# First two units of three feed-forwards by eight plain products, and shorter pauses in the table work

## The chip, the cores and the metric

The kernel runs on one core of a Trainium2 chip. Its time is the device time of one execution in microseconds (us). TensorE does the matrix products, VectorE and ScalarE the elementwise work, GpSimd (POOL in the profile) elementwise work and the accumulating DMAs, SyncE (SP) issues the plain weight loads.

## The reference

The reference is one inference step of a backbone with two layers, on 512 latent and 128 context tokens of width 1024, in float32. Each layer is a gated feed-forward, a token mixing and a second gated feed-forward, each behind a norm that is scaled and shifted by a modulation:

```
h = modulate(rmsnorm(x, g1), sh1, sc1);  x = x + 0.5 * gate1 * ((silu(gate) * up) @ w_out),  gate, up = split(h @ w_in)
h = modulate(rmsnorm(x, gm), sh2, sc2);  x = x + gate2 * token_mixing(h)
h = modulate(rmsnorm(x, g3), sh3, sc3);  x = x + 0.5 * gate3 * ffn2(h)
```

The hidden width is 2816. The mixing holds attention, a spatial gate and a state space model whose tables (powers of a complex decay, products with B and C) depend on weights alone.

## The kernel before

**Products.** Tokens lie along the free axis in two tiles, A (320 to 639) and B (0 to 319); rows of 128 features lie on the partitions. Each float32 operand is split into a high part (ScalarE, line 199 for weights) and a low part (VectorE, line 207). `mm3` makes one product of a 128x128 weight tile and 320 tokens by three matmuls (lines 623 to 625) and advances a clock of its own, `T`, by 0.41. This clock is counted while the program is written out; it orders instructions and is no time of the chip. `K.run` goes through a list of tasks, loads weights ahead into 24 slots (line 174, SP's queue), adds two weight tiles where an operand is a sum (an accumulating load from GpSimd's queue, line 189) and splits them when they are due.

**A feed-forward.** It has 22 units (128 gate and 128 up columns each) in four or six blocks: BLOCKS gives blocks of 4, 4, 4, 3, 3, 4 units for the first feed-forward of a layer and of 6, 6, 6, 4 for the second. A unit needs a 2x2 block product: weights (gate, up) by input halves (features 0 to 3, 4 to 7), times inputs of tiles A and B. It is made by seven block products of four `mm3` each instead of eight. They need sums of the inputs of A and B: X["11"] and X["21"] are the two feature halves of A, "22" is the second half of B, and "t1" to "t4" are sums over both tiles. After a block's units come its output products (`out_task`), for all eight output tiles and both token tiles; in the last block tile A's are done before tile B's last six.

**The start of a feed-forward.** While A's operands are made by `norm`, B's (`later_operands`, `sums`) need A's. To cover that, the first four units (EARLY) begin with the two products that need A only (`early_task`): products with "11" into a bank, a copy of the bank (line 982), further products with "12" into the same bank. For these products the weights are loaded and split once more. The very first feed-forward, (0,0), is opened differently: its first two units go by eight plain products (`lead_task`, `lead_rest`), and the sums are made afterwards from the finished high and low parts of tile B (`all_x_sums`).

**Work beside the products.** Generators in `self.bg` emit instructions between products. Each yields a pause; `clock` advances a generator when `T` has passed its due time, ones that aren't `hot` only while no hot one (a norm, the sums) is alive. Two of them matter: `ada`, which makes the modulation on VectorE, and `ssm_build`, which makes the tables of the state space model during a layer's first feed-forward. `ssm_build` pauses at its start (line 1182), has a prelude, then works through four quarters of two directions each, on VectorE (CL, lines 1297 to 1304), GpSimd (EP and the angles T, lines 1123 to 1142 and 1335 to 1354), TensorE (lines 1315, 1328) and ScalarE (1330), stores to DRAM from GpSimd's queue, and copies a strip eight times at the end of each quarter (1362). When the last output product of tile A is written out, `done()` advances `ssm_build` to its end at once; then the next stage's norm for A is started, then tile B's last 24 products follow.

Of the kernel before, what the change touches and what calls it, by code (L numbers as in the profile page):

```python
# [20 lines left out]
KD = 8  # L21
# [5 lines left out]
HT = 320  # L27
# [31 lines left out]
class Kernel:  # L59
    def __init__(self, ctx, tc, a, o, depth=NL, stop=None, dbg=None):  # L60
# [11 lines left out]
        self.uid = 0  # L72
        self.stage = "in"
# [354 lines left out]
    def norm(self, l, i, X):  # L428
# [19 lines left out]
        if plain and X == "B":  # L448
            yield from self.later_operands(l, i, pb, pbs)
            return  # L450
# [15 lines left out]
        for n in range(KD + 1):  # L466
            yield 1.3
            jobs = []
            if n < KD:
                k = ks[n]  # L470
                t = xn.pop(n) if n in xn else dest(k)
                if plain:
                    name = PLAIN[X][k // 4]
                    hi, lo = self.xop(name) if name else (None, None)
                    hi, lo = (hi[:, k % 4], lo[:, k % 4]) if name else (None, None)
                else:
                    hi, lo = self.h(0, k, slice(s, e)), self.h(1, k, slice(s, e))
                for (r0, r1, c) in RANGES[X]:
# [5 lines left out]
                    else:  # L484
                        v.scalar_tensor_tensor(t[:, r], self.x[:, k, r0:r1], sc, pb[:, r], op0=ALU.mult, op1=ALU.mult)
                        if plain:
                            nc.scalar.activation(t[:, r], t[:, r], AF.Identity, bias=sh)
                        else:
                            nc.scalar.activation(hi[:, r], t[:, r], AF.Identity, bias=sh)
                            jobs.append((lo[:, r], t[:, r], sh, hi[:, r].bitcast(F32)))  # L490
                if n in VIA_POOL or plain and name:
                    if hi is not None:
                        nc.scalar.activation(hi, t, AF.Copy)
                        jobs.append((lo, t, 0.0, hi.bitcast(F32)))
# [4 lines left out]
            if not plain:  # L499
                self.ready[X] = n  # L500
            elif n:
                k = ks[n - 1]
                name = PLAIN[X][k // 4]
                if name:
                    self.xr[name] = k % 4 + 1
# [10 lines left out]
    def later_operands(self, l, i, pb, pbs):  # L516

        nc, v, g = self.nc, self.nc.vector, self.nc.gpsimd
        s, e = HALF["B"]
        m = self.mod[l]  # L520
        raw = {}
        (r0, r1, c), = RANGES["B"]

        def mod(k):
            return (m[:, c, (3 * i + j) * KD + k:(3 * i + j) * KD + k + 1] for j in (1, 0))

        def ahead(k):
            if k < 4:
                raw[k + 4], raw[k] = (self.spare("xn")[:, :HT] for _ in range(2))
                g.tensor_tensor(raw[k + 4], self.x[:, k + 4, s:e], pbs, op=ALU.mult)  # L530

        def first(k):
            t = raw[k]
            sc, sh = mod(k)
            v.scalar_tensor_tensor(t, self.x[:, k, s:e], sc, pb[:, :HT], op0=ALU.mult, op1=ALU.mult)
            nc.scalar.activation(t, t, AF.Identity, bias=sh)
            sc, sh = mod(k + 4)
            nc.scalar.activation(raw[k + 4], raw[k + 4], AF.Identity, bias=sh, scale=sc)
            nc.scalar.activation(self.xop("22")[0][:, k], raw[k + 4], AF.Copy)

        def low(k):
            hi, lo = (z[:, k] for z in self.xop("22"))
            v.tensor_tensor(lo, raw[k + 4], hi.bitcast(F32), op=ALU.subtract)
            self.xr["22"] = k + 1

        while self.norms["A"] in self.bg:
            self.advance(self.norms["A"])
        ahead(0)
        ahead(1)
        yield from self.sums(raw, first, low, ahead)  # L550

    def sums(self, raw, first, low, ahead):
# [14 lines left out]
        for k in range(4):  # L567
# [11 lines left out]
            low(k)  # L579
# [253 lines left out]
    def ffn_items(self, l, f, nxt, bg, lead=False):  # L833
# [19 lines left out]
        def start_bg():  # L853
# [3 lines left out]
            for mk in bg:  # L857
                work.append(self.spawn(mk(stack)))
# [320 lines left out]
    def ssm_build(self, l, p):  # L1179
# [85 lines left out]
        for qq in range(4):  # L1265
# [93 lines left out]
            for jj in range(8):  # L1359
                if jj % 2 == 0:  # L1360
                    yield 2.0
# [661 lines left out]
```

## Time and profile before

| | us |
|---|---|
| median of 3 runs | 2691.12 (2679.48 to 2693.58) |
| profiled execution | 2688.18 |
| its span | 2686.4 |
| TensorE busy | 2403.6 (89%) |
| VectorE busy | 1946.8 (72%) |
| ScalarE busy | 1121.4 (42%) |
| GpSimd busy | 1031.9 (38%) |

The span runs from the first to the last instruction of one profiled execution. Busy shares are means over all stages. The stages are seen by the tiles and lines: the feed-forward (0,0) lasts from about 70 to 611 us, the mixing of layer 0 to 929, (0,1) to 1392, (1,0) to 1925, the second mixing to 2229, and (1,1) to the end.

### The profile page before, as it was taken

The numbers are of one execution on the slowest core, as the hardware profiler recorded it, in microseconds if no ns is written. First come the engines' busy times: TensorE is split into PE (matmuls) and PEld (weight loads), VectorE is DVE, ScalarE is ACT, GpSimd is POOL, SyncE is SP. The second block draws the span as 40 slices with busy tenths as digits, with TensorE's granted clock in tenths as the row PEclk, the third lists the DMA queues.
The fourth block names the chain that finished last, engine by engine and source line by source line (L and its number), as shares of the span: only waits on it lengthen the run. The fifth ranks groups of instructions, "written<-read, shape, count | busy, mean of one in ns | idle before, by whom it ended". The sixth has DMA issues, their size and how long they took to land. (4 is left out here: it accounts for less than half of the span.)

```text
span 2686.4 us, 46513 instructions
## 1 busy us (share of the span) xinstructions
PE 2403.6 (89%) x16420; PEld 2315.5 (86%) x16420; DVE 1946.8 (72%) x4341; ACT 1121.4 (42%) x2567; POOL 1031.9 (38%) x1915
## 2 busy tenths in 40 slices
PE   6789999937999879999997999999498997999999
PEld 5689998837887779999996898899498886999999
DVE  7899788845857787777778987796466578655555
ACT  5433433414444553535354333335244446443533
POOL 5313665573533341211133365665633335121210
PEclk8899999968999989999998999999699998999999
DMA  6576777724453256866745676776153324664753
GB/s 217 135 190 175 183 189 193 188 64 131 147 159 100 75 127 184 192 188 164 193 135 140 163 191 174 183 197 155 52 167 118 111 66 95 143 144 121 157 124 98
DMA packets 197613, 398.19 MB, mean 148 GB/s; under 512 B 32274, under 2 KB 51826, under 8 KB 197380
## 3 DMA queue, kind: packets, MB, share of 16 engines
q1 hardware_dynamic: 132484, 255.46, 29.3%
q0 software_dynamic: 64896, 139.76, 26.8%
q8 instruction: 130, 2.13, 0.3%
q14 instruction: 103, 0.84, 0.1%
HBM read 372.48 MB, written 23.17 MB: 147 GB/s over the span
## 5 line engine op out<-in xcount | busy, mean ns | idle before, releaser
L623 PE MATMUL mm<-hx,w 128*128 128x320 f32 x2904 | 932.0, 321 | 110.3 <-ACT hid L982 27.8
L624 PE MATMUL mm<-hx,w 128*128 128x320 f32 x2904 | 920.9, 317 | 24.2 <-DVE hx L797 11.9
L625 PE MATMUL mm<-hx,w 128*128 128x320 f32 x2904 | 919.8, 317 | 6.3 <-DVE w L207 6.1
L207 DVE TENSOR_TENSOR w<-w 128x512 fp32r<-128x512 f32 (+1 forms) x922 | 628.6, 692 | 212.7 <-ACT w L199 209.0
L199 ACT ACTIVATE w<-w 128x512 fp32r<-128x512 f32 (+1 forms) x922 | 534.4, 608 | 489.5 <-DVE w L207 209.4
L623 PEld LDWEIGHTS mm<-hx,w 128*128 128x128 f32 x2904 | 562.8, 194 | 131.0 <-ACT hid L982 29.7
L624 PEld LDWEIGHTS mm<-hx,w 128*128 128x128 f32 x2904 | 563.7, 194 | 30.0 <-DVE hx L797 13.1
L625 PEld LDWEIGHTS mm<-hx,w 128*128 128x128 f32 x2904 | 563.2, 194 | 11.0 <-DVE w L207 10.5
L623 PE MATMUL mm<-hid,w 128*128 128x320 f32 x1408 | 442.0, 314 | 23.9 <-DVE x L661 20.2
L624 PE MATMUL mm<-hid,w 128*128 128x320 f32 x1408 | 438.6, 312 | 2.3 <-DVE hid L890 2.1
L625 PE MATMUL mm<-hid,w 128*128 128x320 f32 x1408 | 437.6, 311 | 0.0
L189 POOL DMA_DIRECT2D w<-f1i x176 | 152.7, 990 | 605.9 <-DVE w L207 377.9
L371 DVE SCALAR_TENSOR_TENSOR aj<-ar,sbc 128x1024 bf16<-128x1024 f32 x256 | 314.1, 1227 | 19.0 <-DMA ar<-w_ada 18.3
L661 DVE SCALAR_TENSOR_TENSOR x<-mm,mod,x 128x192 f32<-128x192 f32 (+1 forms) x576 | 232.3, 433 | 116.8 <-PE mm L625 115.9
L623 PEld LDWEIGHTS mm<-hid,w 128*128 128x128 f32 x1408 | 267.3, 190 | 31.2 <-DVE x L661 19.5
L189 POOL DMA_DIRECT2D w<-f0i x168 | 156.6, 1030 | 318.3 <-DVE w L207 260.8
L624 PEld LDWEIGHTS mm<-hid,w 128*128 128x128 f32 x1408 | 267.3, 190 | 4.3 <-DVE hid L890 4.2
L625 PEld LDWEIGHTS mm<-hid,w 128*128 128x128 f32 x1408 | 267.1, 190 | 0.0
L912 ACT ACTIVATE hid<-hid 128x320 f32<-128x320 f32 x158 | 74.6, 472 | 202.9 <-DVE hid L938 148.7
L886 ACT ACTIVATE hid<-hid 128x320 fp32r<-128x320 f32 x176 | 82.7, 471 | 153.3 <-DVE hid L954 76.1
L1803 PE MATMUL mm<-w,hx 128*128 128x256 f32 x480 | 144.2, 301 | 0.0
L1804 PE MATMUL mm<-w,hx 128*128 128x256 f32 x480 | 137.7, 287 | 0.9 <-DVE w L207 0.9
(347 smaller groups left out, 3213.1 us busy)
## 6 DMA issues: line engine op xcount, KB each, us to landing
ar<-w_ada SPq DMA_DIRECT2D x128, 512.0 KB, 4.9
w<-f1i SPq DMA_DIRECT2D x184, 256.0 KB, 4.4
w<-f0i SPq DMA_DIRECT2D x182, 256.0 KB, 4.1
w<-f1i POOLq DMA_DIRECT2D x176, 256.0 KB, 5.2
w<-f0i POOLq DMA_DIRECT2D x168, 256.0 KB, 5.6
w<-f1o SPq DMA_DIRECT2D x96, 192.0 KB, 2.5
w<-f0o SPq DMA_DIRECT2D x64, 256.0 KB, 4.3
w<-wqkv SPq DMA_DIRECT2D x48, 256.0 KB, 4.3
```

Of the source, the lines that this page charges most:

```text
L189: nc.gpsimd.dma_start(raw[r][:, :n], src, accum_op=ALU.add)
L199: nc.scalar.activation(pair[c][0][:, :n], raw[r][:, :n], AF.Copy)
L207: nc.vector.tensor_tensor(lo[:, :n], raw[r][:, :n], hi[:, :n].bitcast(F32), op=ALU.subtract)
L371: nc.vector.scalar_tensor_tensor(jk, r, 1.0, self.sbc[:, c, :], op0=ALU.mult, op1=ALU.mult, accum_out=m[:, c, j * KD + k:j * KD + k + 1])
L623: nc.tensor.matmul(out, hi, rhs_hi, start=start, stop=False, skip_group_check=parts)
L624: nc.tensor.matmul(out, hi, rhs_lo, start=False, stop=False, skip_group_check=parts)
L625: nc.tensor.matmul(out, lo, rhs_hi, start=False, stop=stop, skip_group_check=parts)
L661: nc.vector.scalar_tensor_tensor(self.x[:, m, r0:r1], p[:, r0 - s:r1 - s], self.mod[l][:, c, g * KD + m:g * KD + m + 1], self.x[:, m, r0:r ...
L886: nc.scalar.activation(hid[u, X][0], tmp[src], AF.Copy, scale=sign)
L912: return lambda: nc.scalar.activation(t, t, AF.Silu)
L1803: nc.tensor.matmul(p[:, :256], hh, wh, start=k == 0, stop=False)
L1804: nc.tensor.matmul(p[:, :256], hh, wl, start=False, stop=False)
```

## The change

Three parts, which come together:

1. In the feed-forwards other than (0,0), the first two units of the first block are made by eight block products each, as four tasks: tile A with the first half of the features, A with the second, B with the first, B with the second. In each task the order is feature tile by feature tile, two units by two columns into four banks. EARLY stays at four, counted from the third unit (two in blocks of four). 
2. `norm` makes all eight tiles of B as it makes A's (the first four in the place that later holds "t3"). The sums are made by `all_x_sums` from the finished parts, once the last plain task is begun (`self.whole`); `later_operands` is gone.
3. The pauses of `ssm_build` are multiplied by 0.77, and some are shortened besides: the first of layer 0 from 50 to 40, one from 1.5 to 0.5 in each direction, and at the end of a quarter 4.0 and four times 2.0 become 2.5 and once 1.5.

```
         if plain and X == "B":
-            yield from self.later_operands(l, i, pb, pbs)
-            return
...
+        if plain and X == "B":
+            while not self.whole:
+                yield 0.4
+            yield from self.all_x_sums()
...
             for mk in bg:
-                work.append(self.spawn(mk(stack)))
+                work.append(self.spawn(0.77 * (STEP if w is None else w) for w in mk(stack)))
...
+        def plain_items(us):
+            ps = {}
+            def part(X, h):
+                def fn(w):
+                    done = unit_done(us, X)
+                    self.whole = (X, h) == ("B", 1)
+                    if h == 0:
+                        ps[X] = [self.ps()[:, :HT] for _ in w]
+                    def mm(n, k):
+                        hi, lo = self.lead_x(X, k)
+                        self.mm3(ps[X][n], w[n], slice(k % 4 * 128, k % 4 * 128 + 128), hi, lo, k == 0, k == KD - 1)
+                    for k in range(4 * h, 4 * h + (4 if h == 0 else 2)):
+                        while self.ready[X] < min(KD, k + 3):
+                            self.advance(self.norms[X])
+                        for n in range(len(w)):
+                            mm(n, k)
+                    if h:
+                        while self.ready[X] < KD:
+                            self.advance(self.norms[X])
+                        for n in range(len(w)):
+                            for k in (KD - 2, KD - 1):
+                                mm(n, k)
+                            done(n, ps[X][n])
+                return fn
+            return [("task", [("fi", l, f, u, f"{r}{h + 1}") for u in us for r in "12"], part(X, h), 8 * len(us) * MM3[HT])
+                    for X in "AB" for h in range(2)]
...
                 items.append(("call", lambda: self.enter("in")))
-                units(us, us[:n_early] if b == 0 else [])
+                if b == 0:
+                    items += plain_items(us[:2])
+                    us = us[2:]
+                units(us, us[:EARLY] if b == 0 else [])
...
-        yield 50.0 if l == 0 else 12.0
+        yield 40.0 if l == 0 else 12.0
...
-                yield 1.5
+                yield 0.5
                 T = p.tile([128, 2, 2, 65], F32, tag="T", name="T")
...
-            yield 4.0
+            yield 2.5
             for jj in range(8):
-                if jj % 2 == 0:
-                    yield 2.0
+                if jj == 4:
+                    yield 1.5
```

## Rows read from the trace of the kernel before

**Rows 1.** The page: span, and busy us (share of the span) by engine.
```profile
span 2686.4 us, 46513 instructions
...
PE 2403.6 (89%) x16420; PEld 2315.5 (86%) x16420; DVE 1946.8 (72%) x4341; ACT 1121.4 (42%) x2567; POOL 1031.9 (38%) x1915
```

**Rows 2.** Windows, second matmul of each product alone (L624): stretch, length, PE busy (count).
```profile
552.00:635.00 83.00, 12.82 (x34) 8.38 (x35) 0.61 0.17 52
1883.60:1942.30 58.70, 10.19 (x29) 6.53 (x29) 0.65 0.20 59
929.90:985.20 55.30, 21.85 (x60) 14.11 (x61) 0.75 0.46 94
1392.40:1445.20 52.80, 19.71 (x52) 12.58 (x52) 0.74 0.40 81
2229.60:2285.10 55.50, 21.90 (x64) 13.83 (x64) 0.82 0.48 100
1390.00:1397.00 7.00, 2.99 (x9) 1.60 (x8) 0.95 0.44 97
2300.00:2660.00 360.00, 252.52 (x818) 153.41 (x817) 1.00 0.57 131
1530.00:1860.00 330.00, 211.42 (x676) 128.99 (x676) 0.98 0.72 184
210.00:552.00 342.00, 218.32 (x702) 133.05 (x701) 0.99 0.70 185
```

**Rows 3.** Timeline of TensorE around both ends: start, duration, instruction, [idle before, releaser].
```profile
551.65 0.31 PE L625 MATMUL mm<-hid,w 128*128 128x320 f32 x1
...
595.30 0.64 PE L1315 MATMUL sA<-CL,bbd 128*32 128x128 f32 x4 [20.36 <-DVE CL L1300]
...
623.16 0.64 PE L623 MATMUL mm<-hx,w 128*128 128x320 f32 x1 [11.68 <-ACT hx L489]
...
1908.23 0.64 PE L1315 MATMUL sA<-CL,bbd 128*32 128x128 f32 x4 [18.79 <-DVE CL L1300]
```

**Rows 4.** Timeline of GpSimd: the table work of layer 0.
```profile
345.97 1.30 POOL L1191 DMA_DIRECT2D BC<-sBC  x1
...
459.68 0.94 POOL L1191 DMA_DIRECT2D BC<-sBC  x1
...
554.39 1.79 POOL L1341 COPY T<-ang 128x2 f32<-128x2 f32 x12
...
613.52 4.09 POOL L1362 DMA_DIRECT2D dT<-dst  x8
```

**Rows 5.** Waits of TensorE, 929 to 980 us: total, times, longest.
```profile
PE mm L623 <- ACT hid L982: 9.6, 2, 6.6
PE mm L623 <- ACT hx L560: 5.4, 2, 3.5
...
PE sA L419 <- DVE acc L413: 1.1, 1, 1.1
```

**Rows 6.** Windows, all instructions: PE, PEld, DVE, ACT, POOL busy, PEclk, DMA share, GB/s.
```profile
1530.00:1860.00 330.00, 313.82 (x2100) 307.19 (x2099) 268.91 (x543) 131.42 (x272) 200.41 (x434) 0.98 0.72 184
```

**Rows 7.** Timelines of VectorE and TensorE: the sums of the opening.
```profile
97.90 2.36 DVE L607 TENSOR_TENSOR xn<-hx 128x320 f32<-128x320 f32 x4
...
119.40 0.63 PE L623 MATMUL mm<-hx,w 128*128 128x320 f32 x1 [3.21 <-ACT hx L560]
```

**Rows 8.** Groups by line on GpSimd, 1530 to 1860 us: busy, mean ns, idle before.
```profile
L189 POOL DMA_DIRECT2D w<-f0i x61 | 57.6, 1043 | 79.9 <-DVE w L207 62.7 <-DMA w<-f0i 6.4 <-DVE hid L933 5.9
L1341 POOL COPY T<-ang 128x2 f32<-128x2 f32 x72 | 19.7, 608 | 0.0
```

**Rows 9.** Waits of GpSimd, 1530 to 1860 us: total, times, longest.
```profile
POOL dT L1332 <- ACT ET L1330: 21.3, 5, 9.1
POOL dT L1308 <- DVE CL L1304: 15.3, 5, 6.3
```

More of the change, by code (lines that the diff above doesn't have):

```diff
@@ L72, in __init__ @@
         self.uid = 0
+        self.whole = False
         self.stage = "in"
@@ L447, in norm @@
         plain = i != 1
-        if plain and X == "B":
-            yield from self.later_operands(l, i, pb, pbs)
-            return
         ks = range(KD)
@@ L472, in norm @@
                 if plain:
-                    name = PLAIN[X][k // 4]
-                    hi, lo = self.xop(name) if name else (None, None)
-                    hi, lo = (hi[:, k % 4], lo[:, k % 4]) if name else (None, None)
+                    hi, lo = self.lead_x(X, k)
                 else:
@@ L485, in norm @@
                         v.scalar_tensor_tensor(t[:, r], self.x[:, k, r0:r1], sc, pb[:, r], op0=ALU.mult, op1=ALU.mult)
[L486 to L494, printed above, removed]
+                        nc.scalar.activation(hi[:, r], t[:, r], AF.Identity, bias=sh)
+                        jobs.append((lo[:, r], t[:, r], sh, hi[:, r].bitcast(F32)))
+                if n in VIA_POOL:
+                    nc.scalar.activation(hi, t, AF.Copy)
+                    jobs.append((lo, t, 0.0, hi.bitcast(F32)))
                 scaled(n + 2)
@@ L498, in norm @@
             pend = jobs
[L499 to L505, printed above, removed]
+            self.ready[X] = n
+            if plain and n and PLAIN[X][(n - 1) // 4]:
+                self.xr[PLAIN[X][(n - 1) // 4]] = (n - 1) % 4 + 1
+        if plain and X == "B":
+            while not self.whole:
+                yield 0.4
+            yield from self.all_x_sums()
     def xop(self, name):
@@ L514, in new_x, with sums @@
             self.xr[n] = 0
[L516 to L552, printed above, removed]
+    def sums(self, raw, first):
         nc, v, g = self.nc, self.nc.vector, self.nc.gpsimd
@@ L578, in sums @@
             yield 1.0
-            low(k)
             if k:
@@ L584, in sums @@
             g.tensor_tensor(t4, t4, l21, op=ALU.add)
-            ahead(k + 2)
             rest = [split(n, k, t) for n, t in (("t1", t1), ("t2", t2), ("t3", t3))]
@@ L607, in first @@
                 v.tensor_tensor(raw[kk], hi.bitcast(F32), lo.bitcast(F32), op=ALU.add)
-        yield from self.sums(raw, first, lambda k: None, lambda k: None)
+        yield from self.sums(raw, first)
     def start_norm(self, nxt, X):
         self.ready[X] = 0
+        self.whole = False
         if nxt[1] != 1:
@@ L1079, in ffn_items @@
         n_b = len(blocks)
-        n_early = 0 if lead else EARLY
         w_in, w_out = self.a[f"f{f}i"], self.a[f"f{f}o"]
@@ L1090, in ffn_items @@
                 self.raws[op(r)] = (src[r[:2]], 512)
-            if lead and u < 2:
+            if u < 2:
                 self.ops[op("21")] = (512, op("p0"), None)
```

1 line of the change is left out of this document (added).

## The prediction

> **What bounds the kernel now.** I read the page's busy shares first: the tensor engine is busy for 89% of the span, VectorE for 72% [rows 1]. So the matrix products set the time, and what can be won is where they stop. I then counted products (three matmuls each) by stretch, by the second matmul of each. In an undisturbed stretch 818 products take 360 us, 0.440 us each [rows 2]; a stretch's loss is its length less 0.440 us per product. Five stretches lose most:
> - End of the first feed-forward of layer 0, (0,0): 83.0 us hold 34 products (15.0 us), 68.0 us lost. Of layer 1, (1,0): 58.7 us hold 29 (12.8 us), 45.9 us lost [rows 2].
> - Starts of the three later feed-forwards: 55.3, 52.8 and 55.5 us hold 60, 52 and 64 products: 28.9, 29.9 and 27.3 us lost, 86.1 together [rows 2].
>
> The timeline of the tensor engine says why the ends stop: after the product of 551.65 it waits 20.36 us for CL, a tile of the table work, and later 11.68 us for the mixing's first input; in layer 1 18.79 us for CL [rows 3]. GpSimd's timeline fills it: 12 copies of the table work at 554.39, and its last strip loads at 613.52 [rows 4]. This is `done()`: the table work isn't finished when tile A's last output product is out, so all that is left is emitted at once, ahead of tile B's last 24 products, and the next norm queues behind it on GpSimd and ScalarE. At a start the waits name the two other culprits: 9.6 us for the copies of the early products out of their banks (L982), 5.4 us for the first sum operands (L560), beside 1.1 us for the norm's square sums [rows 5]. Granted clock there is 0.75 on average [rows 2].
>
> **Part 1, pauses times 0.77.** The pauses count emitted products (0.41 a product), not microseconds, so I can add them up. A quarter (both directions and the strip loads) held 40.0 + 42.5 + 12.0 = 94.5 of pauses; now 39.0 + 41.5 + 4.0 = 84.5, times 0.77 is 65.1. Each pause ends on a whole product, which makes 101.3 of the one and 69.3 of the other. The trace bears out the old value: the second and third quarters of layer 0 begin at 345.97 and 459.68 [rows 4], 113.7 us apart, 1.12 us for each unit.
> - Layer 0, before: 50 + 44 (prelude) + 4 x 101.3 = 499, while `done()` comes 371 after the start (928 products less 24). 129 are left: the last quarter and 28 of the third, which is where the drain of the trace begins (the copies at 554.39 belong to the third quarter's second direction). After: 31 + 34 + 4 x 69.3 = 342, so it ends 29 units (some 32 us) ahead of `done()`.
> - Layer 1: the work is held while norms run. Before 22 + 44 + 405 = 471 against 387, most of a quarter left, as seen. After: held until the sums end, about 39, then 34 + 277 = 350 against 390 (8 more products): 40 units to spare.
>
> So both drains go. What is late next is the plain handing over from one stage to the next: the one between (0,1) and (1,0), which has no drain, has 9 products in 7.0 us, 3.0 us lost [rows 2]; with some 2 us at the lower clock behind it I keep 5 us each. Gain 68.0 + 45.9 - 10 = 103.9 us.
>
> The drained work doesn't vanish, it moves beside products. Table passes (one quarter, one direction) moved in: 2.4 in layer 0, 1.7 in layer 1. Price of one: 1530 to 1860 us holds six passes and loses 330 - 676 x 0.440 = 32.6 us, 210 to 552 another six and 342 - 702 x 0.440 = 33.1 us [rows 2], 5.5 us each with all else that stops the products there. 4.1 x 5.5 = 22.5 us. Besides, passes come 1.46 times as dense. That costs between nothing (VectorE is idle for 61 of those 330 us [rows 6]) and 0.46 x 65.7 = 30 us; I take 7, near the lower end for that idle time. Together 29.5 us. Part 1: -74.4 us.
>
> GpSimd and VectorE do slow each other here: the twelve small copies of the table work took 1.79 us in the drain, 0.15 us each [rows 4], and 0.61 us each beside VectorE's work [rows 8]. The Trainium skill, "SBUF — State Buffer", section "Who interferes with whom", has a rule for it: a VectorE instruction with two SBUF inputs and a GpSimd instruction that reads SBUF take turns on a shared port, and the second waits the first out. The trace agrees in kind; carried through, the rule makes the second rival below (2627 us), where my sum keeps the price that the six passes of each stretch already paid, turns included.
>
> **Part 2, two plain units.** Added: 8 products x 4 blocks = 32 a unit instead of 28, so 8 more products in each of three feed-forwards, 24 x 0.440 = +10.6 us, all on the tensor engine, which is the path. Removed in each: 6 weight splits on ScalarE and VectorE (7 a unit become 4), 8 accumulating loads on GpSimd's queue; off the path, costed at nothing. Added on VectorE: 8 additions a feed-forward that rebuild the raw tiles from high and low parts; four took 2.36 us in the opening [rows 7], so 4.7 us, hidden beside the last plain and the early products; without that cover they would stand in the path of the sums.
>
> What it does to a start: before, tile B's sums had to be ready after 32 products (all need only tile A). Now 32 products need tile A, 32 need plain tile B, and the sums are begun at the 48th product, beside the last 16 of B. In (0,1) and (1,1) four early units (32 products) follow, in (1,0) two (16). The same sums run in layer 0's opening: raw additions from 97.90, the last operand of the first kind let the products go at 119.40 [rows 7], 22 us from the start. In (0,1) and (1,1) there are 16 + 32 products (21 us) until the first sum operand and 1.3 us more until its last slice: no wait to speak of. In (1,0) there are 16 + 16 (14 us) + 1.3: 6 us of wait.
>
> The added wait (the sums hold until the last plain task is emitted) is one in the order of emission: no engine stands on it. It prolongs the time in which the modulation and table work pause, counted above for layer 1. The plain tasks use all four banks twice, so B's first products wait for A's last copy and multiplication, and the early ones for B's: between nothing and the 6.6 us of the longest L982 wait (part of the 9.6); I take 1 us each, as an ordinary bank wait is near the 1.1 us of the square sums [rows 5]. SP's queue: two weight loads fewer in all, in the same order.
>
> What stays at a start, from 28.9: 2.6 us (1.1 for the square sums, and bank and small products around it), 1.5 for tile A's last slices (no row shows it: between nothing and the 3.0 us of a plain handing over [rows 2], the middle), 2 for the banks, 4 for the early copies (9.6 before: ScalarE still holds splits of the sums ahead of them, but no norm scalings), 3 at the lower clock (granted 0.75 of 55.3 us means 27.6 us at 1.2 GHz; about half of it busy, half of that lost, and half of that stays): 13 us. For (1,0): the 3.0 of the handing over, 1 for the slices, 2, 2 (one group of copies), 6 for the sums, 3: 17. Gain 86.1 - 43 = 43.1 us; bounds: nothing stays but the first 2.6 (78), or half the gain (21). Part 2: -43.1 + 10.6 = -32.5 us.
>
> **Sum.** The profiled execution took 2688.2 us, 2.9 under the median of 2691.1. 2688.2 - 74.4 - 32.5 = 2581.3; with a little of the difference to the median I say 2582.
>
> **Rivals.**
> - The starts hardly gain: the copies and sums keep ScalarE and VectorE as full as before, and each start gives back 5 us instead of 14. For it: VectorE was busy with sums for the whole 22 us in the opening [rows 7]. Against: they have 16 to 48 products more of cover. 15 us from the starts: 2688 - 74 - 15 + 11 = 2610.
> - Denser table work gives most of it back: GpSimd's work, moved in and packed closer, stops VectorE, and VectorE the products. Upper ends: 4.1 passes at twice 5.5 (45) and 30 for density: 2688 - 104 + 75 - 32 = 2627; with the first rival's starts, which give 28 less, 2655. For it: in 1530 to 1860 us VectorE is busy for 269 of 330 us and GpSimd for 200 [rows 6]. Against: products ran at 90% of the pace there.
> - The change doesn't do what it says: the table work isn't done in time and layer 0's drain stays: 2688 - 41 + 13 - 32 = 2628. Against: 29 units to spare, by a sum that hits the old drain.
> - Slower than before: GpSimd's queue overflows. It carries the table work and the accumulating weight loads, one behind the other. 1530 to 1860: 200 us busy, 57.6 of it accumulating loads [rows 6, 8]; the rest, 23.8 us a pass, comes every 38 us instead of 55: 63%, with the loads 81%. It also stands waiting for ScalarE (21.3 us) and VectorE (15.3) [rows 9], 6.1 us a pass, 16%: 97%. As the pauses count products, an overfull queue slows the products in proportion over some 600 us of table work. Slower than before needs 107 us of loss, so a queue filled to 118%; at 125% the time would be 2731. Waits shrink when a queue is late, so I hold it unlikely.
>
> **Numbers.** Forecast 0.70, own range 2545 to 2615; starts 0.12; dense table work 0.10; one drain 0.04; overfull queue 0.04. Range for 8 in 10: 2540 to 2640. Half a per cent, about what a measurement tells from no change, is 13 us: faster 0.93 (all but the last case, and 0.03 for mixtures of the middle ones), same 0.03, slower 0.04.
>
> **What would show it.** Right: no tensor wait over 5 us for CL; table passes end before the last output products; the additions of the opening (L607, 8) four times as many; L982 waits under 5 us a start. Wrong: products in 210 to 552 us and in layer 1's table stretch slower than 0.54 us each; waits for weight splits behind accumulating loads; a wait of over 5 us between plain A and plain B.

## The result, and the profile after

The changed kernel takes 2659.45 us (median of 4 runs, 2652.66 to 2667.64) against 2690.6 us of the kernel before in the same session: ratio 0.9893, 95% interval 0.9853 to 0.9933. It is faster, by 31 us and not by 109; the time lies 19 us above the range (2540 to 2640).

The profiled execution of the changed kernel took 2652.66 us. Its page, to be read beside [rows 1]:

```profile
span 2650.9 us, 46542 instructions
...
PE 2415.9 (91%) x16492; PEld 2324.6 (88%) x16492; DVE 1958.7 (74%) x4355; ACT 1099.2 (41%) x2517; POOL 1049.6 (40%) x1888
```

TensorE has 72 matmuls more, the 24 products of part 2. Windows of the second matmul (now L579), as in [rows 2]: the table work of both layers, then the three starts.

```profile
210.00:588.00 378.00, 223.12 (x710) 136.59 (x709) 0.97 0.69 176
1500.00:1860.00 360.00, 211.75 (x669) 130.38 (x670) 0.95 0.69 176
914.80:979.50 64.70, 32.27 (x97) 20.51 (x97) 0.87 0.40 88
1376.20:1433.50 57.30, 29.01 (x87) 18.15 (x87) 0.87 0.39 86
2196.10:2258.00 61.90, 31.26 (x96) 19.48 (x97) 0.92 0.42 94
```

At 0.440 us a product the two table stretches lose 65.6 us each. Each holds eight passes (a pass is one direction of one quarter): 8.2 us a pass, where the six passes of before lost 5.5 each [rows 2]. A product takes 0.532 and 0.538 us there, just under the 0.54 that the prediction named as a sign of being wrong. The starts lose 22.0, 19.0 and 19.7 us, 60.7 together, where 86.1 were lost and 43 were to stay.

Adding up by stage shows where every microsecond went. The stages are the times from the first product of one to the first of the next in TensorE's timeline, taken at its second matmul; the opening begins at 29 us. "Tables" runs from the second block of a first feed-forward to its last output products; "end" from there to the first product of the mixing; a start is the mixing and the first block of units behind it, for (1,0) that block alone; "opening" is the first block of (0,0); what is not listed stays within a few us.

```
                     opening tables0  end0  (0,1) (1,0) tables1  end1  (1,1)
before                 147.8   356.2  92.8  406.9  80.5   391.9  73.0  391.5
after                  158.1   391.4  33.4  404.7  72.5   426.5  31.7  387.2
e1 pauses alone        159.1   391.9  33.4  402.1  84.0   411.0  31.6  394.7
e2 units alone         150.2   355.0  92.8  404.5  73.0   400.9  78.2  394.5
e3 after, no chain     157.0   358.4  33.4  402.6  72.5   387.5  31.7  392.0
e9 before, no chain    148.2   349.2  70.8  404.4  80.6   375.8  59.1  393.7
e13 chain paced        157.2   377.7  41.2  402.9  72.3   412.7  32.2  393.5
e10 once, SP           157.4   358.7  33.4  399.5  72.6   401.5  31.7  395.7
e11 e10, old units     157.9   361.7  33.4  403.0  85.6   409.8  31.7  390.8
e17 best               158.4   356.5  33.4  393.9  72.9   396.0  31.7  387.1
```

Before to after: the ends give 59.4 + 41.3 = 100.7 us, the starts 2.2 + 8.0 + 4.3 = 14.5; the tables and the opening take 35.2 + 34.6 + 10.3 = 80.1. That is 35.1 us, the difference of the two spans but for 0.4. The ends came as forecast, the starts gave less than half, and the table work took back 80 us where 29.5 were allowed.

The table reads one execution of each kernel, so small differences of (0,1) and (1,1) need care. Kernels with the same code there lie between 399.5 and 407.8 us in (0,1) and between 387.2 and 395.7 in (1,1), and most of that scatter is in the mixings, which no run touches (297.5 to 304.2 and 284.6 to 292.0 us). The first blocks alone, from their first product to their first output product, take 104.4 and 102.8 us before and 103.9 and 101.7 after. So of the 14.5 us of the starts 9.6 lie in the blocks, 8.0 of them at (1,0).

**How the 80 us arise.** Near the middle of a table pass GpSimd makes its rotation powers (the T chain: 12 small copies and 30 small multiplications and additions), and the accumulating weight loads stand in the same queue. GpSimd's timeline of after:

```profile
1561.15 0.86 POOL L190 DMA_DIRECT2D w<-f0i  x1 [3.83 <-DVE w L208]
...
1562.34 4.12 POOL L1330 COPY T<-ang 128x2 f32<-128x2 f32 x12
...
1571.02 0.20 POOL L1114 TENSOR_TENSOR T<-T,tp 128x6 f32<-128x6 f32 x1
1571.30 0.54 POOL L1115 TENSOR_TENSOR tp<-T 128x6 f32<-128x6 f32 x1
...
1572.88 1.19 POOL L1113 TENSOR_TENSOR tp<-T 128x14 f32<-128x14 f32 x1
...
1577.43 1.19 POOL L1115 TENSOR_TENSOR tp<-T 128x30 f32<-128x30 f32 x1
1578.58 0.23 POOL L1116 TENSOR_TENSOR T<-T 128x30 f32<-128x30 f32 x1
...
1582.33 0.89 POOL L190 DMA_DIRECT2D w<-f0i  x1 [0.19 <-issue]
...
1587.01 0.89 POOL L190 DMA_DIRECT2D w<-f0i  x1
```

Between the loads of 1561.15 and 1582.33 lie 21 us without one. ScalarE waits for just that second load, and TensorE for the bank copies behind the split (timelines of ScalarE and TensorE, after):

```profile
1586.62 0.63 ACT L200 ACTIVATE w<-w 128x512 fp32r<-128x512 f32 x1 [17.07 <-DMA w<-f0i]
1589.10 0.63 ACT L200 ACTIVATE w<-w 128x512 fp32r<-128x512 f32 x1 [1.85 <-DMA w<-f0i]
1589.63 0.42 ACT L860 ACTIVATE hid<-mm 128x320 f32<-128x320 f32 x1
```

```profile
1590.10 0.64 PE L578 MATMUL mm<-hx,w 128*128 128x320 f32 x1 [7.21 <-ACT hid L860]
```

Why the chain is slow stands in VectorE's timeline of the same us:

```profile
1570.64 0.54 DVE L616 SCALAR_TENSOR_TENSOR x<-mm,mod,x 128x320 f32<-128x320 f32 x1
1571.11 0.67 DVE L208 TENSOR_TENSOR w<-w 128x512 fp32r<-128x512 f32 x1
...
1572.77 1.23 DVE L372 SCALAR_TENSOR_TENSOR aj<-ar,sbc 128x1024 bf16<-128x1024 f32 x1
...
1577.32 1.21 DVE L372 SCALAR_TENSOR_TENSOR aj<-ar,sbc 128x1024 bf16<-128x1024 f32 x1
```

A small GpSimd instruction takes 0.20 us beside L616, which reads one of its two tiles from a bank, 0.54 beside the weight split and 1.19 beside the modulation (both read two tiles from SBUF): in these two cases it ends when VectorE's instruction ends. Over the chain's 480 multiplications and additions of this trace the medians are 0.21 us beside L616 (93 of them), 0.60 beside the split (81) and 1.17 beside the modulation (34). This is the rule of the Trainium skill, "SBUF — State Buffer", section "Who interferes with whom", that the prediction weighed and left to a rival: such a pair takes turns for a whole instruction. The trace agrees, to a tenth of a us here. It was so before as well: the chain's multiplications and additions took 10.9 us a pass then and 12.4 now. VectorE itself is hardly slowed: in 210 to 540 us its weight split took 0.718 us on average before and 0.720 after, its modulation 1.233 and 1.237. Only the multiplications and subtractions that make CL grew, from 0.45 us to 0.50, in layer 1 to 0.65, some 4 us there in all.

The waits say that the queue had become late. GpSimd standing at an accumulating load until VectorE's split lets it go, 210 to 540 us, before and after (total, times, longest):

```profile
POOL w L189 <- DVE w L207: 80.5, 21, 12.1
```

```profile
POOL w L190 <- DVE w L208: 20.5, 7, 8.6
```

With the waits at these loads that are put down to other instructions it is 82.5 us before and 49.5 after; in layer 1, 1530 to 1860 us, 79.8 and 32.1. A queue that stood at its loads, ready too early, now often reaches them when they could have gone before. In return ScalarE waits for them, 210 to 540 us, before and after:

```profile
ACT w L199 <- DMA w<-f0i: 40.9, 19, 5.7
```

```profile
ACT w L200 <- DMA w<-f0i: 80.6, 35, 12.9
```

The loads themselves are no slower: from issue to landing the median of w<-f0i in GpSimd's queue is 5.6 us before and 5.5 after.

### The profile page after: what moved, and what is told of

Its sections match the earlier page's. It is cut to its first block, busy times and chain, and to the rows that moved or that the text cites. A ratio compares the mean times of both kernels' runs of the same rounds, so it can differ in the third digit from the quotient of the medians.

```text
span 2650.9 us, 46542 instructions
## 1 busy us (share of the span) xinstructions
PE 2415.9 (91%) x16492; PEld 2324.6 (88%) x16492; DVE 1958.7 (74%) x4355; ACT 1099.2 (41%) x2517; POOL 1049.6 (40%) x1888
## 5 line engine op out<-in xcount | busy, mean ns | idle before, releaser
L579 PE MATMUL mm<-hx,w 128*128 128x320 f32 x2928 | 928.1, 317 | 19.3 <-DVE hx L752 10.0
L200 ACT ACTIVATE w<-w 128x512 fp32r<-128x512 f32 (+1 forms) x904 | 525.4, 608 | 540.5 <-DMA w<-f0i 196.4
L578 PEld LDWEIGHTS mm<-hx,w 128*128 128x128 f32 x2928 | 569.1, 194 | 141.0 <-ACT hid L860 34.9
L579 PEld LDWEIGHTS mm<-hx,w 128*128 128x128 f32 x2928 | 569.5, 195 | 24.3 <-DVE hx L752 11.8
L580 PEld LDWEIGHTS mm<-hx,w 128*128 128x128 f32 x2928 | 568.8, 194 | 23.5 <-DVE w L208 23.5
L579 PE MATMUL mm<-hid,w 128*128 128x320 f32 x1408 | 437.7, 311 | 2.3 <-DVE hid L845 2.1
L190 POOL DMA_DIRECT2D w<-f1i x160 | 142.0, 1019 | 579.3 <-DVE w L208 368.0
L372 DVE SCALAR_TENSOR_TENSOR aj<-ar,sbc 128x1024 bf16<-128x1024 f32 x256 | 315.5, 1233 | 20.6 <-DMA ar<-w_ada 19.7
L616 DVE SCALAR_TENSOR_TENSOR x<-mm,mod,x 128x192 f32<-128x192 f32 (+1 forms) x576 | 231.4, 431 | 110.3 <-PE mm L580 109.8
L579 PEld LDWEIGHTS mm<-hid,w 128*128 128x128 f32 x1408 | 266.6, 189 | 4.5 <-DVE hid L845 4.5
L190 POOL DMA_DIRECT2D w<-f0i x160 | 147.2, 1016 | 232.1 <-DVE w L208 121.7
```

The costliest lines, as they stand in the source:

```text
L190: nc.gpsimd.dma_start(raw[r][:, :n], src, accum_op=ALU.add)
L200: nc.scalar.activation(pair[c][0][:, :n], raw[r][:, :n], AF.Copy)
L372: nc.vector.scalar_tensor_tensor(jk, r, 1.0, self.sbc[:, c, :], op0=ALU.mult, op1=ALU.mult, accum_out=m[:, c, j * KD + k:j * KD + k + 1])
L578: nc.tensor.matmul(out, hi, rhs_hi, start=start, stop=False, skip_group_check=parts)
L579: nc.tensor.matmul(out, hi, rhs_lo, start=False, stop=False, skip_group_check=parts)
L580: nc.tensor.matmul(out, lo, rhs_hi, start=False, stop=stop, skip_group_check=parts)
```

## The experiments

Theory Q: GpSimd's queue is late, so accumulating loads, ScalarE's splits, bank copies and products are late one after the other. Rival V: VectorE, or the port that it shares with GpSimd, is full and the queue only looks late. Times are medians; the kernel before lay between 2685 and 2691 us in every session, and "ratio" is to it.

**The parts alone.** e1_pauses is the kernel before with part 1 only, e2_plain the changed kernel with the old pauses:

```diff
 e1: -work.append(self.spawn(mk(stack)))
     +work.append(self.spawn(0.77 * (STEP if w is None else w) for w in mk(stack)))   (and the four pauses of the diff)
 e2: the same lines back
```

> The kernel before with part 1 alone (pauses times 0.77 and the shortened ones). From the stage times of the two traces, part 1 is worth 14 us at the end of (0,0) and 7 us in (1,0). Theory (the parts add up): 2670 us, 20 us under before. Rival (the gain of part 1 needs the later sums of part 2, or the plain units are hurt by it): under 10 or over 30 us gained.

> The changed kernel with the old pauses, so part 2 alone. Theory (the parts add up): the three starts gain 25 us, 24 more products cost 10.6: 2676 us, 14 us under before; both drains are there again with a wait of some 20 us for CL. Rival (shorter pauses eat what the starts gain): over 25 us gained.

e1_pauses 2658.74 us, ratio 0.9902 (0.9868 to 0.9936): all of the change's gain. e2_plain 2693.47, ratio 1.0024 (1.0007 to 1.0041): part 2 alone costs 6 us. The table shows where: two of its starts are 2.4 and 7.5 us shorter, but the third is 3.0 longer, and layer 1's tables and end 9.0 and 5.2. Why these grow beside the old pauses no run shows.

**The chain left out, and the stores moved.** e3_no_chain replaces each complex multiplication of the chain (six instructions) by one memset, so the values of T are left out of the computation; e4_sp_stores issues the table stores and strip loads from SP's queue:

```diff
 e3: -self.cmul(T[:, 0, :, n + 1:n + 1 + q], T[:, 1, :, n + 1:n + 1 + q], ..., eng=gp_)
     +gp_.memset(T[:, :, :, n + 1:n + 1 + q], 0.5)
 e4: -gp_.dma_start(S["T1"][qq, d, :, :512], ...)
     +nc.sync.dma_start(S["T1"][qq, d, :, :512], ...)      (T2, strip and strip loads likewise)
```

> The changed kernel, but each complex multiplication of the angle table T on GpSimd (6 instructions, five times a pass) is replaced by one memset; the table's values are left out. Theory (GpSimd's queue is late, so accumulating weight loads land late, and ScalarE stands on a weight split with the bank copies behind it): some 11 us of GpSimd work a pass go, the loss in the table stretches falls from 8.2 to about 5 us a pass, 16 passes: 2610 us, and ScalarE's wait for accumulated weights in layer 1's stretch falls from 94 to near the 49 us of before. Rival (VectorE is what is full; it keeps all its work): 2645 us or more, the waits for weights hardly less.

> The changed kernel with the table work's stores and strip loads issued from SP's queue instead of GpSimd's. Theory (GpSimd's queue): 39 us of issuing and 45 us of waiting at its head leave the queue in layer 1's 330 us, so the loss a pass falls to about 6 us: 2625 us. Rival (VectorE is what is full): 2655 us, no change. Other rival (the stores' waits now hold up the weight loads in SP's queue): slower than 2660 us, with ScalarE waiting for plain loads.

e3_no_chain 2584.34 us, ratio 0.9627 (0.9595 to 0.9658), 75 us under the changed kernel, more than expected. Its tables are back at 358.4 and 387.5 us, those of before, at the new density. ScalarE's waits in 210 to 540 us:

```profile
ACT w L200 <- DMA w<-f0i: 32.7, 25, 4.1
```

e4_sp_stores 2643.95, ratio 0.9853 (0.9809 to 0.9898): just under half of the expected gain.

**Less chain, or the chain elsewhere.** e5_chain_once makes it once a quarter for both directions; e6_chain_vector gives its multiplications to VectorE:

```diff
 e5: -c = [T[:, i, :, n:n + 1].to_broadcast([128, 2, q]) for i in range(2)]
     +if d == 0:
     +    c = [T4[:, i, :, n:n + 1].to_broadcast([128, 4, q]) for i in range(2)]
     ...
 e6: -T[:, 1, :, 1:1 + q], c[0], c[1], t3[:, :, :q], eng=gp_)
     +T[:, 1, :, 1:1 + q], c[0], c[1], t3[:, :, :q], eng=v)
```

> The T chain of the table work is computed once a quarter for both directions, in instructions of four rows instead of two: half as many GpSimd instructions for the same elements; two small tiles share memory to make room. Theory Q (GpSimd's queue runs late, so the accumulating weight loads in it come late, ScalarE stands at a weight split, the bank copies behind it are late and TensorE stops): leaving the chain out gave 75 us; an instruction of four rows costs more than one of two but less than two, so about a third of that comes back: 2635 us (2615 to 2650). Rival V (VectorE and its port are the limit, GpSimd's queue only looks late): VectorE has the same work, 2655 to 2665.

> The multiplications of the T chain go from GpSimd to VectorE, nothing is left out. Theory Q: GpSimd's queue is rid of them as it was where they were left out (2584); VectorE, busy for 72% of the table stretches, takes some 30 small instructions a pass more, which costs a few us a pass at most: 2605 us (2590 to 2630), and ScalarE's waits for w<-f0i fall to about 40 us a stretch. Rival V: VectorE is the limit, so 16 passes of some 5 us more work slow the kernel: 2680 us or more, and the products wait for DVE.

e5_chain_once 2618.33 us, ratio 0.9747 (0.9721 to 0.9772). e6_chain_vector 2630.69, 0.9789 (0.9754 to 0.9825). Window 210 to 540 us of e6_chain_vector, all instructions, as in [rows 6]:

```profile
210.00:540.00 330.00, 303.63 (x2023) 292.38 (x2022) 299.51 (x795) 123.13 (x258) 160.46 (x314) 0.98 0.71 184
```

VectorE is at 91% there and the kernel still 29 us faster: that VectorE was full falls. (This run takes work off the port too; against the port holding VectorE up stand the durations above, 0.718 and 0.720 us a split.) But VectorE's work is not free either, 46 us stay against leaving the chain out.

**Asking earlier.** e8_adds_early asks for the accumulating loads up to 4 units (10 products) earlier:

```diff
-if due(c, lead + ADD_LAG) and can_add(c) and (
+if due(c, lead + ADD_LAG + 4.0) and can_add(c) and (
```

> The accumulating weight loads are put into GpSimd's queue up to 4 units (some 4.4 us) earlier; the same instructions otherwise. Theory Q: what makes ScalarE stand is that these loads lie behind table instructions in the queue, so asking earlier gives back part of it: 2640 us (2625 to 2652), ScalarE's waits for w<-f0i in 210 to 540 us fall from 80 to under 55. Rival: the loads can't start earlier, because the high part that must precede them (split by ScalarE and VectorE) isn't there, and GpSimd only stands at them longer: 2657 to 2675.

2660.03 us, ratio 0.9902 (0.9873 to 0.993): nothing. Theory Q's number was wrong; ScalarE's waits stayed at 71 us. Either Q was false, or the queue is late by more than those 4.4 us.

**Was it the density?** e9_before_no_chain takes the same memsets into the kernel before, so T's values are left out there too.

> The kernel before (old pauses, old units) with the T chain's multiplications left out (one memset each instead; the values of T are left out of the computation). It asks whether a table pass had this price already when passes came 55 us apart. Theory Q (density: GpSimd stood waiting for 147 of 330 us there, so the chain fitted in between): of the 75 us that leaving it out gave the changed kernel, only the drains' share and a little of each pass comes here: 2660 us (2645 to 2675), and ScalarE's waits for w<-f0i in 210 to 540 us fall by less than 15 from 41. Rival (the chain costs some 4.7 us a pass at any density, so that moving passes out of the drain was mispriced and density costs nothing): twelve passes beside products and the drains' share, 2620 us or less.

2629.03 us, ratio 0.9784 (0.9759 to 0.981): 31 us under expectation. The stage table separates it: 35.9 us of it are the two ends, where the chain stood on the path alone; beside products leaving it out gives 7.0 + 16.1 us, 1.9 for each of some twelve passes. In the changed kernel (e3_no_chain) it gives 33.0 + 39.0, 4.5 for each of sixteen. The expectation had undervalued the ends. The chain alone accounts for the dearer pass: 2.6 us more, where a pass went from 5.5 to 8.2.

**The pace of the chain.** From its first copy to the start of its store the chain took 16.3 to 23.8 us before (11 passes beside products, 20.5 on average) and 15.4 to 24.1 after (16 passes, 19.5). It was asked for in 32 products before (some 16 us), and in 24 now (some 13 us). e13_chain_paced gives the changed kernel the old pauses inside the chain, for three quarters of four:

```diff
-                yield 0.5
+                slow = 1.0 / 0.77 if qq < 3 else 1.0
+                yield 1.5 * slow if qq < 3 else 0.5
 ...
-                    yield 1.5
+                    yield 1.5 * slow          (at each pause of the chain)
```

> The changed kernel with the old pauses inside the T chain alone, in the first three quarters (33 products from its start to its store instead of 25, and the pause ahead of it); all other pauses stay. The same instructions, the table work ends some 27 units later, still about when the last output products of tile A are out. Asking for the accumulating loads 4 units earlier had changed nothing, which a queue that is up to 10 us late explains: the chain takes GpSimd 16 to 24 us and is asked for in 11 to 13. Theory P (the pace of the chain makes the queue late): 12 of 16 passes get back most of what the density cost them, 4.5 less 1.9 us each: 2630 us (2620 to 2642), and ScalarE's waits for w<-f0i in 210 to 540 us fall from 80 to under 60. Rival (the amount of GpSimd's work in the whole pass counts, not its pace): 2655 to 2665.

2628.68 us, ratio 0.9788 (0.9768 to 0.9808), with the very same instructions. The tables are 13.7 and 13.8 us shorter, 2.3 for each of twelve passes, though 7.8 came back at the first end. (By the profiled executions, 2637.20 against 2652.66 us, the gain is 15.5 us; by medians it is 31.) ScalarE's waits, in 210 to 540 us, fell less than expected:

```profile
ACT w L200 <- DMA w<-f0i: 69.2, 29, 8.7
```

The longest is down from 12.9 to 8.7 us, though, and it is the long ones that reach TensorE: of 11.5 us of waits for L860, 6.2 are left. By medians the slower pace gives back 31 of the 75 us that leaving the multiplications out gave. But the edit does two things: it slows the chain by 8 products a pass, and with the longer pause ahead of it the passes of these quarters come 1.29 times as dense as before instead of 1.46. It does not separate the burst from the load of the whole pass; e16_spread, below, does, and gives less.

**The starts.** In the changed kernel TensorE's longest waits at (0,1), 914.8 to 985 us, are again for the early copies, 9.7 us as in [rows 5]; ScalarE's timeline shows the last copy behind the splits of the sums (L516), which wait for VectorE and GpSimd:

```profile
PE mm L578 <- ACT hid L937: 9.7, 2, 6.0
```

```profile
970.25 1.43 ACT L516 ACTIVATE hx<-xt 128x320 fp32r<-128x320 f32 x3 [3.75 <-DVE xt L532]
...
973.84 0.47 ACT L516 ACTIVATE hx<-xt 128x320 fp32r<-128x320 f32 x1 [1.50 <-POOL xt L539]
974.21 0.42 ACT L937 ACTIVATE hid<-mm 128x320 f32<-128x320 f32 x1
```

e7_early_one makes one group of the four early units:

```diff
-for u in early[:3], early[3:]:
+for u in (early,) if len(early) <= 4 else (early[:3], early[3:]):
```

> The four early units in (0,1) and (1,1) are one group instead of three and one, so that their bank copies come once, at the end. Theory: the two waits for early copies (3.67 and 5.99 us at (0,1), 3.67 and 5.57 at (1,1)) come of copies behind the sums' splits in ScalarE's queue; with one group one of the two goes at each start: 2651 us, -8 (2646 to 2656). Rival: the sums' slices are what is late at this place, and the wait moves to the first sum operand: 2657 to 2662.

2657.65 us, ratio 0.9899 (0.9864 to 0.9934): nothing. The waits moved, as TensorE's waits of the same stretch show:

```profile
PE mm L578 <- ACT w L200: 4.6, 1, 4.6
PE mm L578 <- DVE hid L845: 3.2, 1, 3.2
```

**Both cuts, and what part 2 is worth then.** e10_once_sp joins the single chain with SP's stores; e11_once_sp_old_units is the same without the plain units; e12_once_sp_vector puts the single chain's multiplications on VectorE.

```diff
 e10: e5's edit and e4's    e11: the same on the kernel before with e1's pauses
 e12: -T4[:, 1, :, 1:1 + q], c[0], c[1], t3[:, :, :q], eng=gp_)
      +T4[:, 1, :, 1:1 + q], c[0], c[1], t3[:, :, :q], eng=v)
```

> Chain once a quarter, and the table stores and strip loads issued by SP's queue: two cuts of GpSimd's work together. Theory Q: what GpSimd is spared adds up as long as its queue is late; SP's stores alone gave 15 us, the single chain 41; the queue is already less late, so about two thirds of the 15 come on top: 2608 us (2600 to 2616). If the single chain has already made the queue punctual: 2616 to 2622.

> The same two cuts and the new pauses, but with the units of before (no plain units, 24 products fewer). It prices part 2 where the table work is out of its way. Theory: the three starts lose 25 us less with the change and 24 products more cost 10.6, so part 2 is worth some 14 us: 2622 us (2615 to 2630) against e10_once_sp's 2608. Rival: part 2 is worth nothing, as beside the old pauses, where it was 6 us slower: within 4 us of e10_once_sp, or below it.

> As e10_once_sp, with the multiplications of the single chain on VectorE. Theory Q with a second limit: GpSimd is spared another 60 us in all, but VectorE, busy for 81 to 84% of the table stretches, takes them; where the chain went to VectorE whole it cost 46 us against leaving it out. Half of the instructions cost half: about 2605 us, equal to e10_once_sp within 8. If GpSimd's queue alone counts: 2585 to 2592. If VectorE alone counts now: 2620 or more.

e10_once_sp 2599.26 us, ratio 0.9674 (0.9649 to 0.9699); e11_once_sp_old_units 2619.02, 0.9742 (0.9719 to 0.9764); e12_once_sp_vector 2604.03, 0.9685 (0.9665 to 0.9705). Moving the single chain's multiplications gains nothing more: what GpSimd is spared VectorE pays, as expected. And part 2 is worth 20 us once the table work is out of its way: at (1,0) 13.0 us in the first block, and 8.3 more in the tables behind it; (0,1) is 3.5 us shorter and (1,1) 4.9 longer, both within the scatter. Beside the late queue the (1,0) start had gained 11.5 (e1_pauses to after) and the tables had lost 15.5. ScalarE's waits in 210 to 540 us of e10_once_sp:

```profile
ACT w L200 <- DMA w<-f0i: 30.5, 17, 6.9
```

**The pace of the sums.** Two changes to e10_once_sp: e14_sums_fast shortens the pauses inside the token sums, e15_adds_gpsimd gives the additions that rebuild raw tiles to GpSimd.

```diff
 e14: -yield 1.2 / 1.0 / 1.0 / 1.5 / 1.0      +yield 0.6 / 0.4 / 0.4 / 0.8 / 0.4
 e15: -v.tensor_tensor(raw[kk], hi.bitcast(F32), lo.bitcast(F32), op=ALU.add)
      +self.nc.gpsimd.tensor_tensor(raw[kk], hi.bitcast(F32), lo.bitcast(F32), op=ALU.add)
```

> e10_once_sp with the pauses inside the token sums halved or less (1.2, 1.0, 1.0, 1.5, 1.0 to 0.6, 0.4, 0.4, 0.8, 0.4). At (0,1) of the changed kernel the sums ran from 939.92 to 974.8, 35 us, where the opening's took 22. Theory (the sums are late because they are asked for late, a step for every few products, while products stand): asked for faster they end some 5 us earlier, at three starts: 2587 us (2580 to 2593). Rival (VectorE, ScalarE and GpSimd pass the sums to each other, and their splits stand ahead of the early copies): asked for earlier they only fill ScalarE's queue ahead of the copies: 2596 to 2606.

> e10_once_sp with the eight additions a start that rebuild the raw tiles on GpSimd (busy for 5 to 10 of 15 us there) instead of VectorE (11 to 13 of 15). Theory (VectorE's load sets the length of the sums): 4 us less of it at each of three starts, most of that comes back: 2590 us (2584 to 2595). Rival (the sums are a chain of short steps between three engines; GpSimd's additions take longer, 0.9 to 1.2 us against 0.6, and lie ahead of its own part of the chain): 2598 to 2608.

e14_sums_fast 2619.33 us, ratio 0.9747 (0.9729 to 0.9764): 20 slower, and worse than even its rival had it; the opening is 5.9 us longer, the first blocks of (0,1) and (1,1) 6.1 and 2.6. e15_adds_gpsimd 2611.29, 0.9709 (0.9689 to 0.9729): 12 slower, these two blocks 4.9 and 2.8 us longer. Both theories fall. If asking faster costs, asking slower may pay. e16_spread first spreads the single chain (its pauses 2.5 in the direction that holds it, 0.5 in the other); e17_spread_sums_slow adds longer pauses in the sums (1.6, 1.3, 1.3, 2.0, 1.3); e18_sums_slow has these alone, in the changed kernel.

```diff
 e16: -yield 1.5                              +yield 0.5 if d else 2.5      (six pauses of the chain)
 e17, e18: -yield 1.2 / 1.0 / 1.0 / 1.5 / 1.0    +yield 1.6 / 1.3 / 1.3 / 2.0 / 1.3
```

> e10_once_sp with the single T chain of a quarter spread out: its six pauses grow from 1.5 to 2.5 in the first direction, which holds the chain, and fall to 0.5 in the second, where nothing of it is left; the sum stays about the same. Theory P (pace of the chain), which gave 31 us for the doubled chain of the changed kernel: ScalarE's waits for w<-f0i were down to 30.5 and 21.2 us, so there is less to win: 2590 us (2582 to 2597). Rival (the queue is punctual already, or the second direction, now denser, gives it back): 2597 to 2606.

> e16_spread with the pauses inside the token sums a third longer (1.6, 1.3, 1.3, 2.0, 1.3). Faster sums had cost 20 us against e10_once_sp, since their splits stood ahead of the copies and norms in ScalarE's queue; if the pace matters to both sides the best may lie beyond the present one. Theory R (the steps of the sums in ScalarE's queue hold the copies): each start gains 1 to 3 us, 2584 us (2578 to 2590) where e16_spread gives 2590. Rival (the pace of the kernel before is the best; slower sums make the products wait for operands): 2593 to 2605, 4 to 12 above e16_spread.

> The changed kernel with the pauses inside the token sums a third longer and nothing else. It asks whether the pace of the sums cost the change itself some of its starts, or only showed once the table work was out of the way (e17_spread_sums_slow was 13 us faster than e16_spread, 8 of them at the start of (0,1), 3 at (1,1)). Theory R (the sums' splits in ScalarE's queue hold the early copies, whatever the table work does): the starts lie outside the table stretches, so the same 11 us come here: 2648 us (2641 to 2653). Rival (beside the late table work of (1,0) the slower sums delay the queues further and take it back): 2655 to 2663.

e16_spread 2590.46 us, ratio 0.9646 (0.9616 to 0.9676), 9 under e10_once_sp, though the intervals overlap; the tables are 6.3 and 1.5 us shorter. As a quarter is as long as in e10_once_sp, this is what spreading the chain alone gives. e17_spread_sums_slow 2577.53, 0.9592 (0.9566 to 0.9618): 13 us less; the first blocks of (0,1) and (1,1) are 4.9 and 6.2 us shorter. e18_sums_slow 2644.88, 0.9839 (0.9814 to 0.9864), 15 us under the changed kernel by medians, 4.2 by the profiled executions (2648.45 against 2652.66 us); the first blocks of (0,1) and (1,1) are 5.2 and 3.9 us shorter in its trace. TensorE's wait there, 914.8 to 985 us:

```profile
PE mm L578 <- ACT hid L937: 6.5, 2, 5.9
```

e17_spread_sums_slow beats both kernels: 110 us under the one before in its own session, 82 under the changed one's median.

## Why the prediction was wrong

- **Ends: right.** Forecast 103.9 us, measured 100.7. The unit sum that put the table work 29 units ahead of `done()` held: GpSimd's last table store of layer 0 in the changed kernel is at 562.15 and the last strip loads end by 571, and some 25 us later the last output product of tile A is out.

```profile
562.15 0.84 POOL L1345 DMA_DIRECT2D dT<-rot  x1
...
569.84 0.51 POOL L1351 DMA_DIRECT2D dT<-dst  x1 [0.68 <-DMA w<-f0i]
```

- **Table passes: the step that failed.** "4.1 x 5.5 = 22.5 us" and, for density, "I take 7, near the lower end for that idle time": 29.5 us forecast, 80.1 measured, 50.6 of the error's 71.8 us (profiled spans). The price of 5.5 was read where the chain was asked for in 16 us, and the idle time that I looked at was VectorE's. That was the wrong engine: VectorE grew no fuller (266 of 330 us in 210 to 540, 277 before), GpSimd's queue grew late. e3_no_chain and e9_before_no_chain show that the chain in that queue makes the dearer pass; how much of it comes of the burst and how much of the load of the whole pass stays open (e13_chain_paced changes both, e16_spread the burst alone, beside a lighter queue). The pauses by themselves cost 54.8 us in the tables (e1_pauses: 35.7 + 19.1), not 29.5; 15.5 more in layer 1 came only with part 2 (e1_pauses to after), which the sum had at nothing. About 10 of the 80 lie in the opening, which the sum left out: TensorE waits there for VectorE, 13.3 us at 140 to 187 us, 5.7 before. This comes with the pauses (12.1 us in e1_pauses, 5.8 in e2_plain), though VectorE was as full before (44.0 of 47 us, 44.6 now); which instructions do it no run tested. Even the upper ends (45 + 30) were 5 us short.
- **Starts: half right.** No wait stands between plain A and plain B, and the 24 products are there. But "4 for the early copies" was 9.7 at (0,1), and the cover was measured against 22 us, the opening's time from the raw additions to the last operand of the first kind; at (0,1) the same took 31 us (939.92 to 970.7), between other work, and the sums ended at 974.8. 60.7 us stay instead of 43; e17_spread_sums_slow and e18_sums_slow show that the pace of the sums held a good part. Net of the products the starts gave 14.5 us of 32.5, of which 4.9 lie in mixings that the change doesn't touch; in the first blocks of (0,1) and (1,1) the gain does little more than pay for the added products. e2_plain shows that part 2 alone gave nothing.
- **The sum.** It treated the parts as independent. They are not: part 2 is worth -6 us beside the old pauses, 0 beside the new ones and 20 once the table work is lighter. That GpSimd's queue decides this is argued, not shown: beside the old pauses, where it stood at the loads as long as before (e2_plain: 79 us in 1530 to 1860), part 2 lost as well.
- **Rivals.** "Denser table work gives most of it back", with the first rival's starts, gave 2655 us, 4.5 us from the measured time. The two had chances of 0.10 and 0.12, mixtures of the middle cases 0.03. The number is luck in part: that rival had GpSimd's work stop VectorE and VectorE the products, but VectorE's split and modulation kept their length. The sum for the overfull queue (97%) pointed at the engine, and I dismissed it because GpSimd's waits would shrink; they did (at the loads from 82.5 to 49.5 us in 210 to 540 us, from 79.8 to 32.1 in 1530 to 1860), and with them went the lead of the loads.
- **Small readings.** The passes moved in layer 0 are 2.5 by the prediction's own 129 units, not 2.4, and the granted clock of the three starts is 0.77 on average, not 0.75. Neither changes the account. And its rows show GpSimd slowed by VectorE, not each by the other.

## What to carry to other kernels

When background work is emitted by pauses that count another engine's work, compare each burst of it, and the load of a whole pass, with the time that its own queue needs for it: here a burst that was asked for in 13 us and took 20 delayed the loads behind it, though GpSimd was busy for only 68 to 71% of the two table stretches. Before packing it closer, look for what latency-critical work shares that queue, and read the waits of that work's consumer; a queue that stops waiting at its loads is no longer early. And a stall that has several causes in a row moves when one of them is taken away: grouping the early copies gave nothing here (e7_early_one), a slower pace of the sums 15 us (e18_sums_slow).

## What had not been expected of the hardware

- A small GpSimd instruction takes 0.20 us or 1.19 us, by what VectorE runs beside it at that moment; a VectorE instruction with one operand from a bank did not slow it (median 0.21 us beside L616), and VectorE's weight split and modulation did not grow longer.
- Shorter pauses in the token sums made the kernel 20 us slower, pauses a third longer made it 13 us faster (e14_sums_fast against e10_once_sp, e17_spread_sums_slow against e16_spread).
- With the chain's multiplications on VectorE at 91% the products ran faster than with GpSimd's queue late and VectorE at 81% (2023 matmuls in 330 us against 1935).
